# Two of four token tiles turned by VectorE's 32x32 blocks and a trip through DRAM: the second norm of a sparse-attention block

## The chip, the cores and the metric

The kernel runs on one core of a Trainium2 chip. The metric is the time of one execution on the device in microseconds, the median of several runs. The profile is one further execution, taken by the hardware profiler; its times are microseconds from the span's start.

## The reference

The block is a decoder layer for 512 tokens of width 2048: a mixer with native sparse attention, a SwiGLU FFN, an RMSNorm ahead of each and one at the end. What matters here lies between the mixer's output projection and the FFN's first product.

```python
def rmsnorm(x, g):
    y = x32 * lax.rsqrt(jnp.mean(x32 * x32, axis=-1, keepdims=True) + RMS_EPS)
    return (y * g.astype(jnp.float32)).astype(x.dtype)

h = h + nsa_mixer(hn, ...)             # ends in o @ w_out, o: 512 x 2048
h = h + swiglu(rmsnorm(h, ffn_norm_g[i]), ffn_w_in[i], ffn_w_out[i])
```

## The kernel before

**Numbers as two parts.** TensorE multiplies in a format with fewer bits than float32, so each operand is split into a high and a low part, and three products are added (`three`, L344 to L346). ScalarE makes the high part by a copy into the narrower format, VectorE the low part by a subtraction. Weights come in granules of 128x1024: SP loads a granule (L86), ScalarE copies it (L102), VectorE subtracts (L103). `W.take(n)` hands out the next granule and sees that n more are split; `W.ahead(n)` splits n granules ahead and issues the loads that follow. There are three raw and four split buffers, and extra places (`wr_h`, `wr_l`) for six granules.

**Order.** Every engine's instructions are written out in program order; nothing is scheduled for the kernel. An instruction that waits holds up all behind it on its engine. The queues for transfers are SP, ScalarE's and GpSimd's (POOL in the rows), each in order too.

**The output projection.** `acc` (128 tokens x 4 tiles x 2048) is loaded with x. The columns 1024 to 2047 are done first, in two column blocks of 512 (`cb` 2 and 3), for heads 0 to 11: six granules each, for each granule all four token tiles. Then `add` (L1030) adds the four PSUM banks to `acc`, and the spilled sums of the columns 0 to 1023 (`back`, from `d_h`) are added. Then comes the loop over the token tiles t, with heads 12 to 15: for each tile four column blocks of 12 products of 512 columns. `out_tiles` gives four banks, two from `psx` and two named `po`; each has one buffer, so a block writes the bank that the same block of the tile before (or of the column block before) had, and must wait until VectorE's `add` has read it.

**The second norm.** In that loop each block's columns are squared and summed (ScalarE, L1086), the residual is stored to `d_r` by GpSimd (L1082), the factor of each token comes from `rstd` (six small steps, VectorE and one square root on ScalarE), and `scaled` (L314) multiplies by the factor and by ffn_g (`gb2`, ffn_g on all partitions) into the one buffer `xn`. TensorE turns `xn` in the next tile's column blocks 1 and 2, eight 128x128 transposes each (`turned`, L322), so that the 2048 channels lie on partitions; ScalarE (L328) and VectorE (L333) split the result out of PSUM into `n2_hl`. Tile 3 is turned in the first FFN products, which begin with the tokens of tiles 0 and 1.

`ready_made` is a generator of transfers on GpSimd's queue: it makes sums of FFN weights in DRAM (`d_w`), by turns two plain copies of 512 KB and two that accumulate onto them.

The attention turns its probabilities in another way, which the change uses for two tiles: VectorE turns each 32x32 block (L919), four SP transfers write to DRAM with the blocks in a new place (L921), one reads them back (L925).

Of the kernel before, what the change touches and what calls it, by code (L numbers as in the profile page):

```python
# [10 lines left out]
F32 = mybir.dt.float32  # L11
F32R = mybir.dt.float32r
I32 = mybir.dt.int32
AF = mybir.ActivationFunctionType
OP = mybir.AluOpType
# [4 lines left out]
S, D, H, DH, G, HPG = 512, 2048, 16, 128, 4, 4  # L20
NT, KC = S // 128, D // 128
# [6 lines left out]
N_SPILL = 4  # L28
NF = DFF // 128
N_PLAIN = 3  # L30
N_TAIL = 4
G1, G2 = tuple(range(1, 11)), tuple(range(11, 21))
PASSES = [(0, (7, 8, 9, 10, 1, 2, 3, 4, 5, 6), (6, 7, 8, 9, 10)),
# [123 lines left out]
def granules(w_in, w1k, w1v, w_out, f_in, f_out):  # L157
# [46 lines left out]
    off.update((len(out) + i, 0) for i in range(4))  # L204
    for p in range(N_PLAIN):
        out += [(4, 256, [(0, 256, mat(f_in, 512 * i, 4, ffn_col(p), 256, 2 * DFF))]) for i in range(4)]
# [9 lines left out]
def nsa_block(ctx: ExitStack, tc: tile.TileContext, x, rel_bias, mix_g, ffn_g, fin_g, w_in, w_out,  # L216
              pos_k, w1k, w2k, pos_v, w1v, w2v, f_in, f_out, onehot, out):
    nc = tc.nc
    mm, act, dve, pool = nc.tensor.matmul, nc.scalar.activation, nc.vector, nc.gpsimd
# [6 lines left out]
    dram = ctx.enter_context(tc.tile_pool(name="dram", bufs=1, space=DRAM))  # L226
# [5 lines left out]
    W = Weights(nc, rawp, convp, specs)  # L232
    W.at, W.off = 48, off

    ident = const.tile([128, 128], F32, name="ident")
# [6 lines left out]
    d_o = [dram.tile([4, 128, S], F32, name=f"d_o{i}") for i in range(3)]  # L242
    d_h = dram.tile([S, 256 * N_SPILL], F32, name="d_h")
    d_r = dram.tile([NT, 128, D], F32, name="d_r")
    d_a = dram.tile([NF // 2, 128, 5 * S], F32, name="d_a")
    d_w = {j: dram.tile([128, 4, 2, 256], F32, name=f"d_w{j}") for j in G1 + G2}

# [32 lines left out]
    ready_made = made_ahead()  # L280

    def tok(t):
        return slice(128 * t, 128 * (t + 1))
# [22 lines left out]
    def rstd(ss):  # L306
        y = smallp.tile([128, 1], F32, name="rs")
        run(rstd_steps(ss, y))
        return y

    def scaled(src, y, gb, dst):
        for j in range(4):
            c = slice(512 * j, 512 * (j + 1))
            dve.scalar_tensor_tensor(dst[:, c], src[:, c], y, gb[:, c], op0=OP.mult, op1=OP.mult)  # L314
# [112 lines left out]
    with ExitStack() as st1:  # L427
# [11 lines left out]
        with ExitStack() as st0:  # L439
# [86 lines left out]
            p = bank([128, 512])  # L526
            for i in range(N_WARM):
                nc.tensor.transpose(p[:, 128 * (i % 4):128 * (i % 4 + 1)], ident, ident)
            p = bank([128, KC])
# [29 lines left out]
            for q in range(4):  # L559
# [23 lines left out]
                if q == 3:  # L583
                    p = bank([128, S])
# [100 lines left out]
        for i in range(8):  # L685
            g = W.take()
            for t in range(NT):
# [4 lines left out]
                if i == 7:  # L692
                    act(ge[:, t], ps[t][:, 256:304].rearrange("p (n h) -> p n h", n=3), AF.Exp,
                        scale=yneg[:, t:t + 1])
                    v_out(ps[t][:, :256], t, VV[0][0][:, t], VV[0][1][:, t])
            if i == 1:
                p = ps1.tile([128, 128], F32, name="tr")
# [27 lines left out]
        p = ps1.tile([96, G, 128], F32, name="tr")  # L725
# [293 lines left out]
    n2_hl = hn_t  # L1019
    resid = ctx.enter_context(ExitStack())  # L1020
    accp = resid.enter_context(tc.tile_pool(name="accp", bufs=1))
    ps3 = early.enter_context(tc.tile_pool(name="ps3", bufs=4, space=PSUM, side="right"))
    acc = accp.tile([128, NT, D], F32, name="acc")
# [20 lines left out]
    with tc.tile_pool(name="n2", bufs=1) as n2:  # L1044
        act(warm, epsc, AF.Sqrt)
        gb2 = n2.tile([128, D], F32, name="gb2")
        nc.scalar.dma_start(gb2, ffn_g[0:1, :].to_broadcast([128, D]))
        xn = n2.tile([128, D + 64], F32, name="xn")
        wr_h = n2.tile([128, 6, 1024], F32R, name="wr_h")
        wr_l = n2.tile([128, 6, 1024], F32R, name="wr_l")  # L1050
        for i in range(6):
            W.place[marks[0] + i] = wr_h[:, i], wr_l[:, i]
        for cb in (2, 3):
            po = out_tiles()
            cs = [slice(256 * c, 256 * (c + 1)) for c in (2 * cb - 4, 2 * cb - 3)]
            parts = [n2.tile([128, 1024], F32, name="back", bufs=3).rearrange("p (t c) -> p t c", t=NT) for _ in cs]
            for i in range(6):
                if i == 2:
                    for c, p in zip(cs, parts):
                        nc.sync.dma_start(p, d_h[:, c].rearrange("(t p) c -> p t c", p=128))  # L1060
                w = W.take(2 if cb == 2 else min(2 + i, 6))
                for t in range(NT):
                    tokmajor(po[t], w, heads(i), i == 0, i == 5, t)
            W.ahead(3)
            for t in range(NT):
                add(t, cb, po[t])
            for c, p in zip(cs, parts):
                dve.tensor_tensor(acc[:, :, c], acc[:, :, c], p, op=OP.add)
        w8 = []
        for t in range(NT):  # L1070
            ss = smallp.tile([128, 4], F32, name="ss4")
            po = out_tiles()
            for cb in range(4):
                for i in range(2):
                    if t == 0:
                        w8.append(W.take(7 - len(w8)))
                    tokmajor(po[cb], w8[2 * cb + i], heads(6 + i), i == 0, i == 1, t)
                add(t, cb, po[cb])
                if t == NT - 1 and cb == 3:
                    W.ahead(3)  # L1080
                if cb == 3:
                    pool.dma_start(d_r[t], acc[:, t])  # L1082
                if t and cb in (1, 2):
                    turned(xn, (2 * cb - 2, 2 * cb - 1), t - 1)
                junk = ps3.tile([128, 512], F32, name="pp")
                act(junk, acc[:, t, 512 * cb:512 * (cb + 1)], AF.Square, accum_out=ss[:, cb:cb + 1])  # L1086
            next(ready_made)
            scaled(acc[:, t], rstd(ss), gb2, xn)
            W.ahead(min(t, 2))
        firstp.close()  # L1090
        pf0 = ctx.enter_context(tc.tile_pool(name="pf0", bufs=2, space=PSUM))
        pa = [ps3.tile([128, 512], F32, name="pp") for _ in range(2)]
        gs = []
        for i in range(4):
            gs.append(W.take(min(2, 3 - i)))
            run(ws(pa, i, gs[i], 0, 256, of=n2_hl))
            if i in (1, 2):
                turned(xn, (2 * i - 2, 2 * i - 1), 3)
        act(warm, epsc, AF.Silu)
# [94 lines left out]
    def load_unit(q):  # L1194

        p, u = N_PLAIN + q // 2, q % 2
        v = []
# [62 lines left out]
    def merge(p):  # L1260

        A, B, C, F = banks.pop(p)
        p += N_PLAIN
        e = E[p] = ep.tile([128, 6, 256], F32, name="E")
# [15 lines left out]

    NQ = 2 * (2 * NF // 2 - N_PLAIN)
    with tc.tile_pool(name="tmp", bufs=1) as tmp:
# [7 lines left out]
        for i in range(4):  # L1290
            run(ws(pa, i, gs[i], 256, 512, start=False, end=end, of=n2_hl))
            W.ahead(min(i + 1, 3))
            some(1 if i < 3 else 2)
        for p in range(N_PLAIN):
            if p:
                pa = [ps3.tile([128, 512], F32, name="pp") for _ in range(2)]
                end = plain_out(p, pa)
                for i in range(4):
                    w = W.take()
                    if i == 0 or i == 2 and p < N_PLAIN - 1:  # L1300
                        next(ready_made)
# [9 lines left out]
        for u in range(2):  # L1311
            k = slice(8 * u, 8 * u + 4)
# [105 lines left out]
    ss = [late2.tile([128, 4], F32, name=f"sf{t}") for t in range(NT)]  # L1418
# [59 lines left out]
    def tail_load(i):  # L1478

        n = NU - N_TAIL + i  # L1480
        a_hl[n] = [x[:, 48:48 + 2 * S] for x in (slot_tile(), slot_tile())]
        nc.sync.dma_start(f32(a_hl[n][1]), d_a[UNITS[n][1]][:, :1024])

    def tail_split(i):
        h, l = a_hl[NU - N_TAIL + i]
        act(h, f32(l), AF.Copy)
# [69 lines left out]
    for s, (b, js, _) in enumerate(PASSES):  # L1556
# [6 lines left out]
        for i, j in enumerate(units):  # L1563
            left = len(units) - 1 - i
            if n + 3 < NU - N_TAIL:
                load_x(n + 3)
            load_form(n)
            if pending is not None:
                o = accb["now"] = late2.tile([128, NT, 512], F32, name="accb")
# [42 lines left out]
        if last_pass:  # L1612
            two = [slot_tile(F32)[:, 48:1072].rearrange("p (t c) -> p t c", t=2) for _ in range(2)]
            merge_sums(pending, two)
            acc = [x[:, t] for x in two for t in range(2)]
            continue
        o = accb["now"]
# [53 lines left out]
    for t in range(NT):  # L1671
# [16 lines left out]
        y = rstd(ss[t])  # L1688
# [39 lines left out]
```

## Time and profile before

| | us |
|---|---|
| median of 3 runs | 2101.22 |
| lowest, highest | 2100.24, 2101.4 |
| the profiled execution's own time | 2101.66 |
| its span, first to last instruction | 2099.9 |
| TensorE busy in it | 2077.9 |
| VectorE busy | 1627.9 |
| ScalarE busy | 948.8 |

The mean granted TensorE clock is 0.998 of full speed. Products are pipelined: the time from the start of one to the start of the next is what it costs, not its duration.

### The profile page before, as it was taken

Reading aid. Unit: us, or ns where it says so; the run is one execution under the profiler, and the core shown is the slowest. Engines: PE = TensorE matmul, PEld = TensorE weight load, DVE = VectorE, ACT = ScalarE, POOL = GpSimd, SP = SyncE. Lnnn points to the kernel's source line nnn. Section 1 sums busy time; section 2 is a strip of 40 time slices with the busy share of each in tenths; the row PEclk is TensorE's granted clock in tenths of the full one; section 3 lists DMA queues with packets and bytes.
Section 4 is the critical chain, followed back from the end, with each engine's and each line's share of the span. In section 5 each row is a group of like instructions: output and inputs, shape, how many; then the busy total and the mean of one; then the engine's idle time right before and its main releaser. Section 6 shows DMA issues by size and latency. Waiting matters only on the chain.

```text
span 2099.9 us, 39086 instructions
## 1 busy us (share of the span) xinstructions
PE 2077.9 (99%) x15239; PEld 1954.7 (93%) x15239; DVE 1627.9 (78%) x2705; ACT 948.8 (45%) x1524; POOL 279.8 (13%) x406
## 2 busy tenths in 40 slices
PE   9999999999989999999999999999999999999998
PEld 7898788898979889899999999999999999999997
DVE  5565777777787357898888888888888688697767
ACT  5344455555555334434434344344343465464445
POOL 2000111111101001022222132221211100000000
PEclk9999999999999999999999999999999999999999
DMA  7555667666777658578878778788755686685667
GB/s 232 183 150 153 186 190 197 193 192 192 204 221 210 242 171 221 152 203 236 212 205 227 204 223 221 193 236 209 198 158 156 209 267 184 191 298 152 193 204 278
DMA packets 320902, 427.68 MB, mean 204 GB/s; under 512 B 39787, under 2 KB 248875, under 8 KB 320076
## 3 DMA queue, kind: packets, MB, share of 16 engines
q1 hardware_dynamic: 259964, 291.65, 44.3%
q0 software_dynamic: 59856, 131.69, 26.0%
q8 instruction: 119, 1.95, 0.4%
q10 hardware_dynamic: 896, 1.84, 0.2%
q14 instruction: 67, 0.55, 0.1%
HBM read 363.12 MB, written 130.13 MB: 235 GB/s over the span
## 4 chain that ended last, share of the span: by engine, by line
PE 67%; DMA 1%; DVE 1%; ACT 0%; issue 0%; SPq 0%; DVEq 0%; ACTq 0%
PE f L345 18%; PE f L344 18%; PE f L346 18%; PE proj L344 2%; PE proj L346 2%; PE proj L345 2%; PE pp L345 1%; PE pp L346 1%; PE pp L344 1%; PE po L344 1%; PE po L345 1%; PE po L346 1%; DMA tlo<-d_w 1%; PE pp L322 0%; DMA tlo<-in_ffn_w_out 0%; DMA gt<-in_final_norm_g 0%
## 5 line engine op out<-in xcount | busy, mean ns | idle before, releaser
L103 DVE TENSOR_TENSOR wlo<-raw,whi 128x1024 fp32r<-128x1024 f32 (+2 forms) x223 | 247.4, 1111 | 122.9 <-ACT whi L102 122.4
L102 ACT ACTIVATE whi<-raw 128x1024 fp32r<-128x1024 f32 (+2 forms) x223 | 215.9, 971 | 219.9 <-PE f L346 62.2
L344 PE MATMUL f<-hn_h,whi 128*128 128x256 f32 x984 | 271.6, 276 | 0.0
L346 PE MATMUL f<-hn_h,wlo 128*128 128x256 f32 x984 | 271.6, 276 | 0.0
L345 PE MATMUL f<-hn_l,whi 128*128 128x256 f32 x984 | 271.6, 276 | 0.0
L1220 ACT ACTIVATE whi<-raw 128x1024 fp32r<-128x1024 f32 x123 | 126.1, 1057 | 303.0 <-DVE raw L1116 299.6
L1116 DVE TENSOR_TENSOR tlo<-tt,thi 128x1536 fp32r<-128x1536 f32 (+1 forms) x83 | 145.4, 1752 | 77.3 <-ACT thi L1225 77.1
L344 PE MATMUL proj<-hn_h,whi 128*128 128x512 f32 x512 | 204.2, 399 | 0.7 <-ACT hn_h L486 0.7
L345 PE MATMUL proj<-hn_l,whi 128*128 128x512 f32 x512 | 200.6, 392 | 0.3 <-DVE hn_l L487 0.3
L346 PE MATMUL proj<-hn_h,wlo 128*128 128x512 f32 x512 | 200.6, 392 | 0.0
L345 PEld LDWEIGHTS f<-hn_l,whi 128*128 128x128 f32 x984 | 184.7, 188 | 0.0
L344 PEld LDWEIGHTS f<-hn_h,whi 128*128 128x128 f32 x984 | 184.7, 188 | 0.0
L346 PEld LDWEIGHTS f<-hn_h,wlo 128*128 128x128 f32 x984 | 184.7, 188 | 0.0
L1225 ACT ACTIVATE thi<-tt 128x1536 fp32r<-128x1536 f32 x82 | 121.8, 1486 | 72.9 <-PE f L345 61.3
L344 PE MATMUL f<-thi,slot 128*128 128x256 f32 (+1 forms) x546 | 152.0, 278 | 0.0
L345 PE MATMUL f<-tlo,slot 128*128 128x256 f32 (+1 forms) x546 | 152.0, 278 | 0.0
L346 PE MATMUL f<-thi,slot 128*128 128x256 f32 (+1 forms) x546 | 151.9, 278 | 0.0
L346 PE MATMUL proj<-whi,hn_l 128*128 128x256 f32 (+2 forms) x496 | 145.4, 293 | 3.8 <-DVE hn_l L807 3.8
L1116 DVE TENSOR_TENSOR wlo<-raw,whi 128x1024 fp32r<-128x1024 f32 x123 | 147.0, 1223 | 1.1 <-ACT whi L1220 1.1
L344 PE MATMUL proj<-whi,hn_h 128*128 128x256 f32 (+2 forms) x496 | 145.7, 294 | 0.8 <-ACT hn_h L806 0.8
L345 PE MATMUL proj<-wlo,hn_h 128*128 128x256 f32 (+2 forms) x496 | 144.8, 292 | 0.0
L345 PE MATMUL f<-wlo,slot 128*128 128x256 f32 (+1 forms) x432 | 121.7, 282 | 0.0
(400 smaller groups left out, 6452.1 us busy)
## 6 DMA issues: line engine op xcount, KB each, us to landing
raw<-in_ffn_w_in SPq DMA_DIRECT2D x135, 512.0 KB, 5.3
d_w<-in_ffn_w_out POOLq DMA_DIRECT2D x80, 512.0 KB, 8.5
rawx<-in_ffn_w_in SPq DMA_DIRECT2D x41, 512.0 KB, 5.4
raw<-in_ffn_w_out SPq DMA_DIRECT2D x73, 256.0 KB, 3.8
tlo<-d_w SPq DMA_DIRECT2D x73, 256.0 KB, 4.5
d_a<-d_a POOLq DMA_DIRECT2D x120, 128.0 KB, 6.0
slot<-d_a SPq DMA_DIRECT2D x18, 768.0 KB, 7.5
raw<-in_nsa_w_in POOLq DMA_DIRECT2D x24, 512.0 KB, 5.0
```

The source lines that it names most:

```text
L102: self.nc.scalar.activation(hi[:, :n], src, AF.Copy)
L103: self.nc.vector.tensor_tensor(lo[:, :n], src, hi[:, :n].bitcast(F32), op=OP.subtract)
L344: mm(o, ah, bh, start=start, stop=False, skip_group_check=True)
L345: mm(o, ah, bl, start=False, stop=False, skip_group_check=True)
L346: mm(o, al, bh, start=False, stop=stop, skip_group_check=True)
L1116: dve.tensor_tensor(o, a, b, op=OP.subtract)
L1220: act(h, r, AF.Copy)
L1225: act(h, ttf, AF.Copy)
```

## The change

For token tiles 0 and 1 `turned` and `scaled` are left out. Instead ScalarE copies the tile of `acc` into `xn`, times the token's factor, with the columns in a new order; VectorE turns all 32x32 blocks of `xn` in place; four SP transfers of 256 KB write it to `d_n`, and one of 1 MB reads it back over the tile's part of `acc`, now with channels on partitions. Two tiles later, in column blocks 1 and 2, `landed_split` makes the two parts, eight channel blocks of 128 at a time, one instruction of ScalarE and one of VectorE for each, both times ffn_g, which is a factor of each partition now (`gcol2`). That column is loaded as 16 rows of 128 and turned by TensorE after column block 2 of the first part. Four of the steps of `ready_made` move from the ends of the token tiles to the granules 3 and 5 of the two column blocks. `W.ahead(min(t, 2))` at the end of each tile gives way to one `W.ahead(2)` in tile 0, before its factor is made.

```diff
+BLOCKED = 2
...
+    d_n = [dram.tile([4, 32, 4, 512], F32, name=f"d_n{t}") for t in range(BLOCKED)]
...
         xn = n2.tile([128, D + 64], F32, name="xn")
+        gcol2 = xn[:, D:D + KC]
+        nc.scalar.dma_start(xn[:KC, :128], ffn_g.rearrange("o (k p) -> (o k) p", p=128))
+
+        def blocked(t, y):
+
+            act(xn[:, :D].rearrange("p (m k j) -> p k m j", m=4, j=32),
+                acc[:, t].rearrange("p (k m j) -> p k m j", m=4, j=32), AF.Copy, scale=y)
+            dve.transpose(xn[:, :D], xn[:, :D])
+            for a in range(4):
+                nc.sync.dma_start(d_n[t][:, :, a].rearrange("m j f -> j m f"),
+                                  xn[32 * a:32 * a + 32, :D].rearrange("j (m f) -> j m f", m=4))
+            nc.sync.dma_start(acc[:, t], d_n[t].rearrange("m j a f -> (m j) (a f)"))
+
+        def landed_split(t, ks):
+
+            v = acc[:, t].rearrange("p (a k s) -> p k a s", a=4, s=32)
+            h, l = (x[:, :, tok(t)].rearrange("p k (a s) -> p k a s", a=4) for x in n2_hl)
+            for k in ks:
+                act(h[:, k], v[:, k], AF.Copy, scale=gcol2[:, k:k + 1])
+                dve.scalar_tensor_tensor(l[:, k], v[:, k], gcol2[:, k:k + 1], h[:, k].bitcast(F32),
+                                         op0=OP.mult, op1=OP.subtract)
+
...
             for i in range(6):
+                if i in (3, 5):
+                    next(ready_made)
...
             W.ahead(3)
+            if cb == 2:
+                gp = ps3.tile([128, 512], F32, name="pp")
+                nc.tensor.transpose(gp[:, :KC], xn[:KC, :128], ident[:KC, :KC])
+                dve.tensor_copy(gcol2, gp[:, :KC])
             for t in range(NT):
                 add(t, cb, po[t])
...
-                if t and cb in (1, 2):
+                if t > BLOCKED and cb in (1, 2):
                     turned(xn, (2 * cb - 2, 2 * cb - 1), t - 1)
                 junk = ps3.tile([128, 512], F32, name="pp")
                 act(junk, acc[:, t, 512 * cb:512 * (cb + 1)], AF.Square, accum_out=ss[:, cb:cb + 1])
-            next(ready_made)
-            scaled(acc[:, t], rstd(ss), gb2, xn)
-            W.ahead(min(t, 2))
+                if 2 <= t < 2 + BLOCKED and cb in (1, 2):
+                    landed_split(t - 2, range(8 * cb - 8, 8 * cb))
+                if not t and cb == 3:
+                    W.ahead(2)
+            y = rstd(ss)
+            if t < BLOCKED:
+                blocked(t, y)
+            else:
+                scaled(acc[:, t], y, gb2, xn)
```

## Rows read from the trace of the kernel before

**Rows 1.** The page, busy us, share of the span and instructions.

```profile
PE 2077.9 (99%) x15239; PEld 1954.7 (93%) x15239; DVE 1627.9 (78%) x2705; ACT 948.8 (45%) x1524; POOL 279.8 (13%) x406
```

**Rows 2.** TensorE's waits, whole span: instruction <- releaser: us, times, longest.

```profile
PE proj L346 <- DVE hn_l L807: 3.8, 4, 2.2
PE o L344 <- issue: 3.1, 1, 3.1
```

**Rows 3.** Timeline of TensorE, token tiles: start, us, engine, line, operation.

```profile
760.66 0.39 PE L344 MATMUL proj<-wr_h,hn_h 128*128 128x512 f32 x1
...
771.54 0.39 PE L344 MATMUL proj<-wr_h,hn_h 128*128 128x512 f32 x1
...
776.98 1.03 PE L322 MATMUL pp<-ident,xn 128*128 128x128 f32 x8
...
784.20 0.39 PE L344 MATMUL proj<-wr_h,hn_h 128*128 128x512 f32 x1
...
797.10 0.39 PE L344 MATMUL proj<-wr_h,hn_h 128*128 128x512 f32 x1
```

**Rows 4.** Timelines: the second column block's start on three engines; a 16-row transpose.

```profile
713.70 1.06 ACT L102 ACTIVATE whi<-raw 128x1024 fp32r<-128x1024 f32 x1 [6.18 <-DMA raw<-in_nsa_w_out]
...
725.01 1.28 DVE L1030 TENSOR_TENSOR acc<-acc,proj 128x512 f32<-128x512 f32 x2
...
728.02 0.39 PE L344 MATMUL proj<-whi,hn_h 128*128 128x512 f32 x1
...
5.85 0.23 PE L530 MATMUL mlp<-ident,g 16*128 16x16 f32 x1
...
6.12 0.17 DVE L531 COPY gcol<-mlp 128x16 f32<-128x16 f32 x1 [4.91 <-PE mlp L530]
```

**Rows 5.** Timeline of VectorE around the end of token tile 0.

```profile
763.73 2.35 DVE L103 TENSOR_TENSOR wlo<-raw,whi 128x1024 fp32r<-128x1024 f32 x2
...
773.21 0.16 DVE L293 TENSOR_REDUCE ms<-ss 128x1 f32<-128x4 f32 x1 [0.79 <-ACT pp L1086]
...
774.67 2.74 DVE L314 SCALAR_TENSOR_TENSOR xn<-acc,rs,gb 128x512 f32<-128x512 f32 x4
```

**Rows 6.** Groups by shape, whole span: count, busy us, mean ns, idle before.

```profile
L1691 ACT ACTIVATE slot<-slot,rs 128x1024 f32<-128x1024 f32 x3 | 3.5, 1152 | 2.6 <-DVE rs L304 2.6
...
L919 DVE STREAM_TRANSPOSE p<-p 128x1152 f32<-128x1152 f32 x16 | 22.1, 1379 | 0.6
L919 DVE STREAM_TRANSPOSE p<-p 128x896 f32<-128x896 f32 x16 | 17.8, 1112 | 0.5
...
L942 ACT ACTIVATE pth<-ptr 128x128 fp32r<-128x128 f32 x32 | 9.3, 297 | 4.3 <-DMA ptr<-d_p 4.3
...
L906 ACT ACTIVATE p<-u,mx 128x128 f32<-128x128 f32 x32 | 12.4, 387 | 0.0
...
L946 DVE TENSOR_TENSOR ptl<-ptr,pth 128x128 fp32r<-128x128 f32 x32 | 9.1, 284 | 21.5 <-ACT pth L942 21.5
```

**Rows 7.** Transfers: SP and GpSimd timelines, issues (KB, median us to landing), a window.

```profile
682.32 1.75 SPq L921 DMA_DIRECT2D d_p<-p  x4
687.73 0.52 SPq L925 DMA_DIRECT2D ptr<-d_p  x1
...
772.72 0.56 POOL L1082 DMA_DIRECT2D d_r<-acc  x1 [78.63 <-DVE acc L1030]
...
d_w<-in_ffn_w_out POOLq DMA_DIRECT2D x80, 512.0 KB, 8.5
...
d_r<-acc POOLq DMA_DIRECT2D x4, 1024.0 KB, 5.4
...
gb<-in_ffn_norm_g ACTq DMA_DIRECT2D x1, 1024.0 KB, 8.4
...
704.00:706.00 2.00, 2.00 (x10) 1.68 (x9) 0.00 (x0) 0.00 (x0) 0.00 (x0) 1.00 1.00 416
```

**Rows 8.** A 1 us window after TensorE's longest wait: busy by engine, granted clock, DMA.

```profile
222.00:223.00 1.00, 1.00 (x4) 0.76 (x3) 0.47 (x2) 0.00 (x0) 0.45 (x1) 0.50 0.93 308
```

## The prediction

> **What bounds the kernel now.** I read the page's busy times first: TensorE works 99% of the span [rows 1], so the kernel lasts as long as TensorE's instruction stream plus its waits. The list of TensorE's waits over the span comes next: eight groups, 13.4 us in all, of which the two longest stand in [rows 2]; none lies between 740 and 850 us, where the change works. So an instruction taken out of TensorE there is worth its whole time, and a wait put in costs its whole time. Last came the timeline from 760 to 823 us, by engine. Token tile 0, which turns nothing, takes 771.54 - 760.66 = 10.88 us; tile 1, which turns tile 0, 12.66; tile 2, 12.90 [rows 3]. VectorE and ScalarE have idle time there, but the reader must look at their order, not their share: each takes its instructions in the order in which the kernel writes them, and an add that frees a PSUM bank or a factor that TensorE needs can stand behind an instruction that waits for something else.
>
> **What is removed.** Two tiles' transposes, four sets of eight. By the lengths of the tiles that is (12.66 - 10.88) + (12.90 - 10.88) = 3.8 us of TensorE time. All of it is on the path. The eight copies out of PSUM and the eight VectorE scalings that go with it are hidden today and count for nothing by themselves.
>
> The Trainium skill speaks against this trade: "VectorE: DVE Perf Modes", section "Rules for kernel authors", sends a 128x128 transpose to TensorE if a PSUM destination will do, because VectorE turns 32x32 blocks only. No run before shows the full turn on VectorE; the page gives no time for the detour.
>
> **The ffn_g column.** One 16-row transpose on TensorE after the second column block's products, and a copy of it to SBUF on VectorE ahead of that block's four adds. The same pair at the start of the kernel took 0.23 and 0.17 us [rows 4]. Its place matters more than its length. Today the first add starts at 725.01, while TensorE is still at that block's later tiles, so all banks are free when the next block starts at 728.02. In the new order the add waits for a transpose that comes after all four tiles. The next block's tile 0 writes the bank that this add empties (one buffer for each of the four). So: transpose to 728.3, copy, add from 728.45 for 0.64, TensorE goes on at 729.15, or 1.1 us later than now. Below, the bound is the transpose alone, 0.2; above, 1.4 if copy and add don't overlap. I take 1.1, since the order fixes it.
>
> **The early accumulating DMAs.** Four steps of ready_made (eight DRAM transfers of 512 KB) move from the token tiles into the two column blocks. GpSimd's queue waits from 772.72 - 78.63 = 694 us with nothing in it, so they start there, in a stretch where the DMA engines are already full [rows 7], beside x, the spilled partial sums and w_out. The granule that the next block starts on is converted at 713.70 as soon as it has landed, and is needed at 728.02 [rows 4]; that cover of some 12 us hides them. I cost them at nothing; without the cover it is a rival.
>
> **The new chain, tile 0.** Times are on the old clock, without the 1.1 us. Today the sum of squares is reduced at 773.21 and the factor is there at 774.67 [rows 5]. The change puts two ffn_w_in splits ahead, one conversion of 1.06 [rows 4] and then two subtractions, 2.35 [rows 5], less what overlaps, so the reduction starts at 776.5 and the factor is there at 778.0. ScalarE's scaled copy of 128x2048 is twice the 1152 ns of the 128x1024 row, less one start: 2.1 us (1.9 to 2.3 [rows 6]). The block transpose by VectorE's two rows is 1379 + 896 x 267/256 ns, 2.31 us; 2.45 if it scaled with size [rows 6]. It ends at 782.6. Then four writes of 256 KB on SP. In the attention four writes of the same form and the read behind them were issued 5.4 us apart [rows 7]; I take 5.5, up to the 8.4 of a 1 MB load in a full stretch, not under 4.9. The read of 1 MB back: 5.4, as the store of 1 MB; 4.9 to 8.4 [rows 7]. Tile 0 lands at 793.6. The two ffn_w_in loads that the splits set free stand on SP ahead of the writes and are issued before 778; behind the writes SP has nothing that TensorE needs before tile 3 is over. The store of the residual, which reads the same tile, is issued at 772.72 and takes 5.4 [rows 7], so it holds back nothing.
>
> **Who stands behind it.** VectorE waits for the copy and turns from 778.1 to 782.6, and tile 1's four adds are queued behind that. TensorE would start tile 2 at 771.54 + 10.88 = 782.4 in the bank of tile 1's first add, which ends at 783.3: a wait of 0.9 us.
>
> Tile 1's last add ends at 785.1, its factor is there at 787.5. Its scaled copy writes the same buffer xn, which the four writes free at 788.1; copy to 790.2, transpose to 792.6. Tile 2's first two adds, ready since 786 and 789, are done only at 793.8. Now the split of tile 0, in two halves of eight channel blocks. The nearest rows are ScalarE's 128x128 copies of 297 ns (387 with a per-partition operand) and VectorE's 284 ns [rows 6]; consecutive ones overlap, so I take 0.30 a step, ends 0.22 and 0.39, and VectorE one step behind. The half ends at 797.3. Then, one behind the other: add, square, second half to 801.5, add, square, factor (1.5) to 804.4, and two of the four scalings, 1.4: tile 2's first half of xn is there at 805.8. Today the same half is there at 774.67 + 1.37 = 776.0, and TensorE asks at 776.98 [rows 3, 5]. TensorE asks after tile 3's second block, at 783.3 + 10.88 + 5.44 = 799.6. It waits 6.2 us.
>
> Then the same in small: tile 3's adds and tile 1's split follow the late scaling. The first half of tile 1 ends at 812.9, add and both subtractions of the turned blocks free the bank of the first FFN product at 814.9; TensorE is there at 813.1 and waits 1.8. The second half, add, a split, square, factor and half a scaling end at 821.7; TensorE, two granules further (as many columns each as a block, 2.72), is at 820.3 and waits 1.4. Sum of waits 0.9 + 6.2 + 1.8 + 1.4 = 10.3 us.
>
> **The sum.** -3.8 + 1.1 + 10.3 = +7.6 us. The profiled execution took 2101.66 for its span of 2099.9, so 2109.3; it lies 0.4 above the median of 2101.22, so I forecast 2108.8. With steps of 0.22, DMA times of 4.9 and a copy of 1.9 the waits, walked again, make 6.7 and the sum is +4.0; with steps of 0.39, the read at 8.4, a copy of 2.3 and a turn of 2.45 they make 15.7 and the sum is +13.0. The read is not what binds at 5.4 (tile 0 lands 0.9 before ScalarE turns to it); at 8.4 it adds some 2 us.
>
> **Rivals.** 0.2%, 4.2 us, is about what a measurement of this kernel can tell from no change.
>
> Forecast, waits of serial work on VectorE and ScalarE: 2105.2 to 2114.2, chance 0.65, of which 0.04 under +4.2.
>
> Cover holds: the turns on VectorE delay nobody because the scaling of tile 2 comes in time. What it needs is its first half by 799.6, or 6.2 us sooner than I count. For it speaks that tile 0's DMA trip ends before its use; against it, that every step of the chain behind 792.6 has a row. Price: -3.8 + 1.1, or 2098.5, same. Chance 0.13. That the column's wait doesn't come either and a little more than the sets is gained, 2097.0 or less: 0.07, the only case that is faster.
>
> DMA crowd: the moved transfers hold back the granules at 700 to 728. Each took 8.5 us [rows 7], and they go in four pairs, one pair behind the other, 34 us; if they get half of the engines meanwhile, what SP carries is late by up to 17 us, 5 more than the cover: 2113.8. Chance 0.08.
>
> Clock: after the one TensorE wait of 3.1 us [rows 2] the granted clock stood at 0.50, the 1.2 GHz level, for three slices of 1 us and a part of two more [rows 8]: 3 x 0.50 and 0.2, 1.7 us of work lost. A 6.2 us wait should bring this too. I leave it out of the sum since it falls ahead of the waits of 1.8 and 1.4, which take it up: TensorE only comes less early. If it isn't taken up, +9.3, 2110.5. Chance 0.07.
>
> The Trainium skill, "TensorE: Matmul & The Clock Gate", section "What's actually happening", says the same of the cause: the throttled state is the default and activity releases it. The row agrees, with 0.50 after the wait.
>
> **Chances and range.** Faster 0.07; same 0.13 + 0.04 = 0.17; slower 0.61 + 0.08 + 0.07 = 0.76. The range goes from 2101.5, about half the way from the forecast's low end to the held cover, since a part of the cover can hold, to the forecast's high end of 2114.2. Left out are the two cases of a gain, 0.20.
>
> **What would show it.** TensorE's transposes of xn are 32 instead of 64, and the wait list gets three names between 728 and 830: an add on VectorE (about 1 us twice), a transpose waiting for xn's scaling (about 6), and the first FFN products (1 to 2, twice). The block transposes last 2.3 us, and tile 0's ends some 9 us behind that tile's last square. The granted clock falls once behind the long wait. Wrong would be: tile 2's scaling on time, no wait of over 1 us at the third turn; the trip through DRAM over 14 us; or waits on w_out at 728 to 760.

## The result and the profile after

The changed kernel takes 2118.65 us (median of 5 runs, 2117.42 to 2121.07) against 2101.22 of before: ratio 1.0084, 95% interval 1.0073 to 1.0095. That is slower, as forecast, but by 17.4 us instead of 7.6, and above the range. The profiled execution took 2117.98 us, its span is 2116.2.

The page's busy line of the changed kernel, to be held against [rows 1]:

```profile
PE 2080.3 (98%) x15208; PEld 1954.7 (92%) x15208; DVE 1630.5 (77%) x2724; ACT 958.2 (45%) x1550; POOL 279.5 (13%) x406
```

TensorE's waits of the changed kernel, the four longest groups (sum in us, times, longest). The first two don't stand in the list of before [rows 2]:

```profile
PE proj L346 <- DVE acc L1032: 9.2, 3, 7.7
PE pp L324 <- DVE xn L316: 6.3, 1, 6.3
PE proj L348 <- DVE hn_l L809: 3.1, 3, 2.2
PE o L346 <- issue: 2.7, 1, 2.7
```

Where they stand shows the timeline of TensorE, the first product of each stage with the wait ahead of it in brackets:

```profile
728.17 0.23 PE L1093 MATMUL pp<-ident,xn 16*128 16x16 f32 x1
736.15 0.77 PE L346 MATMUL proj<-whi,hn_h 128*128 128x512 f32 x1 [7.75 <-DVE acc L1032]
...
771.67 0.39 PE L346 MATMUL proj<-wr_h,hn_h 128*128 128x512 f32 x1
...
782.55 0.39 PE L346 MATMUL proj<-wr_h,hn_h 128*128 128x512 f32 x1
...
793.88 0.50 PE L346 MATMUL proj<-wr_h,hn_h 128*128 128x512 f32 x1 [0.29 <-DVE acc L1032]
...
806.28 0.50 PE L346 MATMUL proj<-wr_h,hn_h 128*128 128x512 f32 x1 [1.20 <-DVE acc L1032]
...
818.33 1.94 PE L324 MATMUL pp<-ident,xn 128*128 128x128 f32 x8 [6.27 <-DVE xn L316]
...
828.28 0.28 PE L346 MATMUL pp<-hn_h,whi 128*128 128x256 f32 x1
```

Up to 728 us TensorE runs alike in both kernels. Two losses follow, and the larger one lies ahead of the token tiles, in a stretch that the prediction held for nearly untouched:

- **Column blocks.** The token tiles start at 771.67 instead of 760.66 [rows 3]: 11.0 us. Of these 8.1 lie between the last product of the first column block and the first of the next (728.08 to 736.15, the wait of 7.75 with the 16-row transpose), and 2.9 in the block behind, which runs partly at the lower clock and takes 35.52 us instead of 32.64.
- **Token tiles.** 10.88, 11.33, 12.40 and 22.0 us, 56.6 in all, against 49.3 before, from 760.66 [rows 3] to the first FFN product below: 7.3 us, with the wait of 6.27 for xn that was forecast at 6.2.

```profile
810.00 0.28 PE L344 MATMUL pp<-hn_h,whi 128*128 128x256 f32 x1
```

The sum of the two, 18.3, and some 0.3 over the FFN's first granules make the 18.6 by which TensorE is late at 850 us. The span is only 16.3 longer, since between 1715 and 1775 us the profiled execution of before is itself 1.8 us slower than that of the changed kernel, and than that of eight of the kernels below, the one with the move alone and the one without turns among them. What slows it there isn't known.

The rows below show stretches of 2 us (time, busy us and count of TensorE, its weight loads, VectorE, ScalarE, GpSimd; then the granted clock, the DMA share, GB/s). The granted clock fell to 0.50, the 1.2 GHz level, during or behind each of the two long waits, as behind the one wait of before [rows 8]:

```profile
728.00:730.00 2.00, 0.40 (x3) 0.13 (x1) 0.00 (x0) 0.00 (x0) 0.37 (x1) 1.00 1.12 311
...
732.00:734.00 2.00, 0.00 (x0) 0.00 (x0) 0.72 (x1) 0.99 (x1) 0.00 (x0) 0.50 1.14 217
...
740.00:742.00 2.00, 2.00 (x6) 1.52 (x6) 1.20 (x2) 0.00 (x0) 0.00 (x0) 0.50 0.11 31
...
820.00:822.00 2.00, 2.00 (x7) 1.61 (x6) 1.36 (x3) 1.14 (x4) 0.00 (x0) 0.50 0.00 0
```

Why the first wait is so long stands in three views of the changed kernel. First GpSimd's timeline, the DMA issues from 693.5 to 712 us (KB each, median us to landing) and ScalarE's conversions of w_out:

```profile
694.12 0.66 POOL L256 DMA_DIRECT2D d_w<-in_ffn_w_out  x1
```

```profile
acc<-in_x SPq DMA_DIRECT2D x2, 2048.0 KB, 21.4
d_w<-in_ffn_w_out POOLq DMA_DIRECT2D x6, 512.0 KB, 14.8
...
back<-d_h SPq DMA_DIRECT2D x2, 512.0 KB, 24.0
...
raw<-in_nsa_w_out SPq DMA_DIRECT2D x1, 512.0 KB, 21.9
```

```profile
724.36 1.06 ACT L103 ACTIVATE whi<-raw 128x1024 fp32r<-128x1024 f32 x1 [16.78 <-DMA raw<-in_nsa_w_out]
730.40 1.06 ACT L103 ACTIVATE whi<-raw 128x1024 fp32r<-128x1024 f32 x1 [4.99 <-DMA raw<-in_nsa_w_out]
733.01 1.06 ACT L103 ACTIVATE whi<-raw 128x1024 fp32r<-128x1024 f32 x1 [1.55 <-DMA raw<-in_nsa_w_out]
```

SP's queue belongs to the picture, first of the kernel before and then of the changed one:

```profile
701.46 4.30 SPq L1060 DMA_DIRECT2D back<-d_h  x2
```

```profile
702.90 10.66 SPq L1086 DMA_DIRECT2D back<-d_h  x2
```

Then VectorE's timeline from 724 to 737 us:

```profile
725.45 1.23 DVE L104 TENSOR_TENSOR wlo<-raw,whi 128x1024 fp32r<-128x1024 f32 x1 [16.61 <-ACT whi L103]
731.49 1.23 DVE L104 TENSOR_TENSOR wlo<-raw,whi 128x1024 fp32r<-128x1024 f32 x1 [4.82 <-ACT whi L103]
734.10 1.22 DVE L104 TENSOR_TENSOR wlo<-raw,whi 128x1024 fp32r<-128x1024 f32 x1 [1.39 <-ACT whi L103]
735.24 0.17 DVE L1094 COPY xn<-pp 128x16 f32<-128x16 f32 x1
735.33 1.27 DVE L1032 TENSOR_TENSOR acc<-acc,proj 128x512 f32<-128x512 f32 x2
```

The moved transfers start at 694.12, and a 512 KB load of w_out issued beside them takes 21.9 us. SP is held for 10.66 instead of 4.30 us at the two loads of spilled sums, and the w_out loads behind them are issued from 713.7 us on instead of 705.9. The granule that the next block starts on is converted at 724.36 instead of 713.70 [rows 4] and its subtraction is over at 726.7: its own cover of 12 us did hold. But the splits look ahead. The two granules behind it are converted at 730.40 and 733.01, and their subtractions stand on VectorE ahead of the four adds. The first add begins at 735.33 instead of 725.01 [rows 4], and TensorE waits for the PSUM bank that it empties.

### The profile page after: what moved, and what is told of

It reads as the page before. It is cut to its first block, busy times and chain, and to the rows that moved or that the text cites. A ratio compares the mean times of both kernels' runs of the same rounds, so it can differ in the third digit from the quotient of the medians.

```text
span 2116.2 us, 39098 instructions
## 1 busy us (share of the span) xinstructions
PE 2080.3 (98%) x15208; PEld 1954.7 (92%) x15208; DVE 1630.5 (77%) x2724; ACT 958.2 (45%) x1550; POOL 279.5 (13%) x406
## 4 chain that ended last, share of the span: by engine, by line
PE 62%; issue 2%; DVE 2%; DMA 2%; SPq 1%; ACT 1%; POOL 0%; ACTq 0%; DVEq 0%; POOLq 0%
PE f L347 19%; PE f L346 19%; PE f L348 18%; PE pp L348 1%; PE pp L347 1%; PE pp L346 1%; PE proj L346 1%; PE proj L347 1%; PE proj L348 1%; DMA raw<-in_nsa_w_out 1%; SPq L1086 1%; PE po L346 0%; PE po L347 0%; PE po L348 0%; SPq L87 0%
```

## The experiments

All ratios are against the kernel before, run on the same chip beside each group. "Shift" is by how much TensorE runs behind the profiled execution of before, read by laying the two lists of products side by side.

**Undo the move.** The four `next(ready_made)` out of the column blocks, back to the tile ends:

```diff
-                if i in (3, 5):
-                    next(ready_made)
...
+            next(ready_made)
             y = rstd(ss)
```

> The changed kernel with the four steps of ready_made put back at the ends of the token tiles. Theory 1 (the moved transfers make the w_out granules late, and the adds stand behind the late granules' splits on VectorE): TensorE's wait of 7.7 us at 728 shrinks to the 1.1 us of the ffn_g column's order, and the granted clock stays full there, so 2118.6 - 11.0 + 1.1 = 2108.7 us; up to 2112 if the transfers, back among the tiles, lengthen the trip through DRAM. Rival (the wait comes from the column's transpose and copy ahead of the adds): it stays, 2115 us or more.

2113.97 us, ratio 1.0061 (1.0046 to 1.0076): 4.7 won, not 10, and 2 above what the theory allowed. The column blocks cost only 1.4 now (shift 0.7 at 725 us, 2.1 at 750). But the transfers now run beside the trip through DRAM. ScalarE's and VectorE's timelines of this kernel, and TensorE's wait:

```profile
801.12 2.45 ACT L1069 ACTIVATE hn_h<-acc,xn 128x128 fp32r<-128x128 f32 x8 [3.48 <-DMA acc<-d_n]
```

```profile
801.56 2.39 DVE L1070 SCALAR_TENSOR_TENSOR hn_l<-acc,xn,hn_h 128x128 fp32r<-128x128 f32 x8 [4.75 <-ACT hn_h L1069]
```

```profile
811.90 1.94 PE L324 MATMUL pp<-ident,xn 128*128 128x128 f32 x8 [9.90 <-DVE xn L316]
```

The split of tile 0 waits for its tile to land, and the wait for xn grows from 6.27 to 9.90. So the move does shelter the trip, and pays for it in w_out.

**The move alone,** in the kernel before (the same lines with the signs turned, nothing else):

> The kernel before with only the four steps of ready_made moved into the column blocks; tiles are turned by TensorE as before. Theory 1: the wait at 728 and the fall of the clock come with the move alone, so 2101.2 + 10.5 = 2111.7 us (2109 to 2113). Rival (the wait needs the column's transpose and copy): no change, 2101.2 us, within 1 us.

2109.89 us, ratio 1.0049 (1.0032 to 1.0065): 9.1 us from eight transfers whose data no instruction of this stretch reads. TensorE's longest wait of this kernel, and the order of VectorE:

```profile
735.33 0.76 PE L344 MATMUL proj<-whi,hn_h 128*128 128x512 f32 x1 [6.26 <-DVE acc L1030]
```

```profile
733.36 1.23 DVE L103 TENSOR_TENSOR wlo<-raw,whi 128x1024 fp32r<-128x1024 f32 x1 [1.04 <-ACT whi L102]
734.50 1.28 DVE L1030 TENSOR_TENSOR acc<-acc,proj 128x512 f32<-128x512 f32 x2
```

It is the same picture without the ffn_g column or the turns. The theory holds, and the rival (the column's transpose and copy) falls.

**The adds ahead** of the splits and the ffn_g column, in the changed kernel:

```diff
+            for t in range(NT):
+                add(t, cb, po[t])
             W.ahead(3)
             if cb == 2:
...
-            for t in range(NT):
-                add(t, cb, po[t])
```

> The changed kernel with the four adds of each column block ahead of the split of further granules and ahead of the column's copy; the transfers stay moved. Theory 1 with order as the cause: x lands at 717 and TensorE's first tile is done at 724.5, so the adds run from 725 and the wait of 7.7 us and the clock's fall go: 2118.6 - 11 = 2107.7 us. Rival (the granules themselves are too late for TensorE): a wait on a split of w_out takes its place, 2113 us or more.

2115.29 us, ratio 1.0068 (1.0053 to 1.0083): the direction of the theory, a third of the size, and a time in the rival's range. VectorE's timeline of this kernel:

```profile
731.79 1.23 DVE L104 TENSOR_TENSOR wlo<-raw,whi 128x1024 fp32r<-128x1024 f32 x1 [5.28 <-ACT whi L103]
732.93 1.28 DVE L1032 TENSOR_TENSOR acc<-acc,proj 128x512 f32<-128x512 f32 x2
```

One late subtraction still stands ahead: that of the lookahead inside the block's last `W.take(2)`, not of `W.ahead(3)`. The wait falls from 7.75 to 4.67. Order explains 3 us here; the rest is the late granule, through the subtraction that still stands ahead.

**No turns.** The kernel before without the transposes and splits of tiles 0 and 1, whose tokens the FFN then doesn't get:

```diff
-                if t and cb in (1, 2):
+                if t > 2 and cb in (1, 2):
```

> The kernel before with the turns of tiles 0 and 1 and their two splits left out, so that the FFN's first half works on tokens that were not normalised; nothing is put in their place. It prices the gain by itself. By the tile lengths: 3.8 us less, 2097.4 us. Rival (part of the transposes' time is covered): 2099 us or more.

2097.81 us, ratio 0.9987 (0.9977 to 0.9996). From 775 to 800 us and on the shift goes from 2.16 to -1.55, 3.7 us; the medians differ by 3.0. That is all that the change can win.

**Transfers in the quiet stretch.** They wait behind a GpSimd copy that reads an accumulator column of the first column block's last tile; adds first:

```diff
+            if cb == 2:
+                gate = smallp.tile([128, 1], F32, name="gate")
+                pool.tensor_copy(gate, acc[:, NT - 1, 512 * cb:512 * cb + 1])
+                for _ in range(4):
+                    next(ready_made)
```

> The changed kernel with both harms of the column blocks taken away: the eight accumulating transfers wait (behind one small GpSimd copy that reads the accumulator) until the adds of the first column block are done, and so run in 728 to about 765 us, where neither x nor the spilled sums nor the DRAM trip is under way; and the four adds stand ahead of the split and of the ffn_g column. Theory (the 11.0 us lost ahead of the token tiles are the crowd at 694 and the adds behind the late granules; the 7.3 us in the tiles are serial work on VectorE and ScalarE): only the tiles' part is left, 2100.8 + 7.5 + 0.2 = 2108.5, range 2106 to 2110.5, with no TensorE wait over 1 us at 728 and the wait for xn still near 6.3. Rival (the crowd only moves, the stretch behind 728 isn't quiet enough): 2113 or more, with waits on granules between 728 and 771.

2124.04 us, ratio 1.0111 (1.0096 to 1.0126), far from both. At 850 us the shift is 8.8, about the theory's 7.7; then it grows by 0.35 in every 25 us of the FFN. Three variants that ran beside it had the same new tile: with two idle buffers for tile 1; on top of that with both splits in tile 3; and on top of that with the factors on GpSimd and splits of 512 columns. Their main lines, in this order:

```diff
+            if t:
+                bs = [n2.tile([128, 1024], F32, name="back", bufs=3) for _ in range(2)]
...
-                if 2 <= t < 2 + BLOCKED and cb in (1, 2):
-                    landed_split(t - 2, range(8 * cb - 8, 8 * cb))
+                if t == NT - 1:
+                    landed_split(cb // 2, range(8 * (cb % 2), 8 * (cb % 2) + 8))
...
+            pool.tensor_tensor(v, v, gcol2.unsqueeze(1).unsqueeze(3).to_broadcast([128, 4, KC, 32]), op=OP.mult)
```

> As the gated kernel, but tile 1 is scaled and turned in two idle 128x1024 buffers instead of in xn, so ScalarE no longer waits 4.2 us for the four writes of tile 0; each write becomes two halves. Theory A (the wait for xn is serial work only): the turn of tile 1 ends some 4 us sooner and the wait of 6.3 falls to about 2, 2104.3. Theory B (tile 0's trip through DRAM is next in line: it lands at 795 on the clock of before, while the split would then be asked for at 790.5): half of it comes back as a wait for the landing, 2106.5. Range of both 2103 to 2108.5. If nothing is won (2108.5), the buffer was no link of the chain.

> As the kernel with two buffers, but both tiles' splits stand in token tile 3, behind tile 2's scaling: eight channel blocks in each of its four column blocks. Theory (VectorE's serial work is what binds): tile 2's scaling comes in time and the wait for xn goes; but tile 3 now has 2.75 + 2.6 + 2.6 + 9.8 = 17.7 us of VectorE work against 12.7 of TensorE, so about 6 us come back as waits of the first FFN products: 2100.8 - 3.8 + 6 = 2103, range 2099 to 2107. Rival (the splits fit beside tile 3): 2097 to 2098, faster than before. Second rival (something else than the splits holds back xn): the wait of some 6 us stays, 2108.

> As the kernel with both splits in token tile 3, but the ffn_g factors are applied to the landed tiles by GpSimd in one multiplication each, so that a split is four wide pairs (512 columns) instead of sixteen narrow ones: 5.1 us of VectorE work in tile 3 instead of 9.8. Theory (serial VectorE and ScalarE work binds): the waits of the first FFN products shrink from about 6 to about 3, for the landing of tile 1 and GpSimd's pass over it, 2100.8 - 3.8 + 3 = 2100, range 2097 to 2104. Rival: GpSimd's pass takes longer than 6 us or slows VectorE, and the kernel is no faster than the one with narrow splits.

They took 2120.33, 2124.08 and 2121.08 us (ratios 1.0102, 1.0103 and 1.0096; the four times of the second lie in two pairs, near 2120 and 2128), and for them too only the traces up to 850 us tell something: shifts of 4.9, 13.6 and 4.9. In the second the wait for xn at tile 3 is gone, and waits of 1.68, 1.23 and 2.53 stand behind it, as that theory says; 5.95 more stand at 768 us, behind a w_out granule that ScalarE waited 5.81 for; this was the slowest of its four executions. In the third the factors on GpSimd stop VectorE, as its timeline and GpSimd's show:

```profile
796.93 0.16 DVE L300 RECIPROCAL rs<-rs 128x1 f32<-128x1 f32 x1 [0.27 <-ACT rs L298]
797.13 2.94 DVE L302 SCALAR_TENSOR_TENSOR nt<-rs,ms 128x1 f32<-128x1 f32 x1
```

```profile
796.39 3.67 POOL L1073 TENSOR_TENSOR acc<-acc,xn 128x2048 f32<-128x2048 f32 x1
```

A 128x1 instruction that takes 0.22 us elsewhere lasts 2.94 and ends at 800.07, when GpSimd's multiplication does (800.06). The Trainium skill, "SBUF — State Buffer", section "SBUF: two separate sides", says why: VectorE and GpSimd share a pair of ports, and where a VectorE instruction with two SBUF inputs meets a GpSimd instruction that reads SBUF, the first holds it for its whole instruction and the other is blocked. The rows agree: the blocked one reads `rs` and `ms`, while the reciprocal ahead of it, with one input, took its 0.16 us beside the same multiplication.

**The new tile taken out, and put in alone.** The gate copy now writes an unused column of xn; the same with two buffers; and the kernel before with nothing but an unused tile:

```diff
-                pool.tensor_copy(gate, acc[...])
+                pool.tensor_copy(xn[:, D + 32:D + 33], acc[...])
```

```diff
+    pad = smallp.tile([128, 1], F32, name="pad")
+    pool.memset(pad, 0.0)
```

> The gated kernel again, but GpSimd's small copy goes into an unused column of xn instead of a new 128x1 tile (three buffers, 12 bytes per partition). In the first gated run TensorE stood only 8.8 us behind the kernel before at 850 us, and then lost 0.35 us more in every 25 us of the FFN, with no wait and a granted clock of 1.00. Theory (the new tile moved all later buffers by 12 bytes, and that alone slows the FFN's products): without it the time is 2100.8 + 8.8 = 2109.5, range 2107.5 to 2111.5. Rival (the gated transfers themselves slow the FFN): again about 2124.

> As the gated kernel without the new tile, with two idle 128x1024 buffers for tile 1. In the first such run TensorE stood 4.9 us behind before at 850 us. Theory (ScalarE's wait for tile 0's writes is a link of the serial chain, and nothing else of the change costs): 2100.8 + 4.9 = 2105.7, range 2104 to 2107.5. Rival (the gain of 3.9 is given back later): as the gated kernel, 2109.

> The kernel before, unchanged in all its work, with one unused 128x1 tile (three buffers, 12 bytes per partition) set to zero at the start. Theory (12 bytes of displacement slow the FFN's products by 1.3%): 10.5 us between 890 and 1680 us and some 3 more behind, 2114, range 2110 to 2117. Rival (the drift came from the gated transfers): 2100.8, within 1.5.

All three came as the theories had them: 2110.17 (ratio 1.0051, 1.0034 to 1.0068), 2105.28 (1.0019, 1.0010 to 1.0029) and 2115.96 us (1.0072, 1.0057 to 1.0087). The unused tile, twelve bytes per partition, costs 15 us. The window from 1200 to 1300 us, first of the gated kernel without the tile, then of before with it:

```profile
1200.00:1300.00 100.00, 100.00 (x885) 100.00 (x884) 86.03 (x103) 42.46 (x42) 22.69 (x31) 1.00 0.85 218
```

```profile
1200.00:1300.00 100.00, 100.00 (x873) 100.00 (x872) 86.32 (x104) 38.15 (x37) 23.37 (x35) 1.00 0.74 205
```

885 products against 873 in the same time, both at a clock of 1.00 and without a wait. Laid beside the kernel before, from 890 to 1700 us, the loss of 10.8 us stands almost whole in the 3012 products that read the buffers thi and tlo: 10.35 us, 3.4 ns each. The 4038 others lose 0.5 together.

Against the changed kernel, the gate and the adds' place give back 8.5 us by the medians. The quiet stretch isn't always quiet: in the profiled execution of the gated kernel, the slowest of its five, one w_out granule was late and TensorE waited 6.61 at 770.84. The second buffer gives back 4.9 more: ScalarE scales tile 1 at 786.42 without waiting for tile 0's writes, and the wait for xn falls to 3.98.

**Another order.** From the two-buffer kernel: the turn behind the next tile's second add, tile 0's split in blocks (2, 2) and (3, 0) (tile, block), tile 1's from (3, 2) on and between the quarters of tile 3's scaling, `W.ahead(3)` in tile 3 left to the next take:

```diff
-                if 2 <= t < 2 + BLOCKED and cb in (1, 2):
-                    landed_split(t - 2, range(8 * cb - 8, 8 * cb))
...
+                for tt, cc, b, ks in ((2, 2, 0, range(8)), (3, 0, 0, range(8, KC)), (3, 2, 1, range(4)), (3, 3, 1, range(4, 8))):
+                    if (t, cb) == (tt, cc):
+                        landed_split(b, ks)
+                if t in (1, 2) and cb == 1:
+                    turn(t - 1)
```

> As the kernel with two buffers, with the instructions of VectorE and ScalarE put in another order and no work taken out: the block transpose of a tile stands behind the next tile's second add instead of ahead of its first, the two ffn_w_in splits behind tile 0's scaled copy and turn, and tile 0's split in the third block of tile 2 and the first of tile 3, tile 1's from the third block of tile 3 on and between the quarters of tile 3's scaling. Theory (it is the order of the two queues that costs, not the amount of work up to tile 3): tile 2's scaling is there at 798.4 on the clock of before, asked for at 798.7, so the wait for xn goes; in tile 3 VectorE has 16.5 us of work and some 3 come back as waits of the FFN's first products: 2100.8 - 3.8 + 3 = 2100, range 2097 to 2104. Rival (the amount of work binds wherever it stands): 2105, as the kernel with two buffers.

2108.02 us, ratio 1.0034 (1.0023 to 1.0045): slower than the kernel it came from. Half of the expectation held: no wait for xn is left. But TensorE's timeline has others in its place:

```profile
816.38 0.66 PE L324 MATMUL pp<-ident,xn 128*128 128x128 f32 x4 [2.77 <-DVE hn_l L335]
...
831.81 0.58 PE L348 MATMUL pp<-hn_h,wlo 128*128 128x256 f32 x1 [3.06 <-DVE wlo L104]
```

The clock falls to 0.50 behind each, and the tiles cost 7.2 (shift 10.2 at 775 us, 17.4 at 850), more than with two buffers alone (3.2). The profiled execution is the slowest of nine, 2117.19 us, with one more late granule (a wait of 5.36 at 768.74) ahead of the tiles.

**Transfers in the FFN.** The two-buffer kernel without the gate; the four steps go beside others in the FFN's product units:

```diff
-        for _ in range(PRE[q % len(PRE)]):
+        for _ in range(PRE[q % len(PRE)] + (q in (2, 4, 6, 8))):
```

> The kernel with two buffers, but the four moved steps of ready_made (eight DRAM transfers) go into neither the column blocks nor the token tiles: each is issued beside another step early in the FFN's product units. In the gated kernels single executions had a w_out granule late beside them (6.6 and 5.4 us of wait at 769). Theory: with the transfers out of the way no granule of w_out is late, the column blocks cost 0.2 to 0.4 and the tiles 3.2 to 3.7: 2104.5, range 2102.5 to 2106.5, and a narrower spread than 2103 to 2110. Rival (the transfers only do their harm elsewhere): granules of ffn_w_in late in the FFN, 2108 or more.

2104.54 us, ratio 1.0016 (1.0007 to 1.0025), eleven runs between 2102.9 and 2106.4: the expected time to 0.1, and no w_out granule late. The column blocks cost 0.4 (shift 0.58 at 725 us, 1.01 at 750), and 3.6 are left in the tiles, with a wait for xn of 4.39.

**One tile.** `BLOCKED = 1` on top of that, tile 0 in the idle buffers, its turn behind tile 1's second add, its split in blocks (2, 2) and (3, 0); then the second half moved to (3, 2):

```diff
-                if (t, cb) in ((2, 2), (3, 0)):
+                if (t, cb) in ((2, 2), (3, 2)):
                     landed_split(0, range(8) if t == 2 else range(8, KC))
```

> The change in half its size, with what the runs have taught: only token tile 0 is turned by VectorE's blocks and DRAM (in the two idle buffers), tile 1 by TensorE as before; the turn stands behind tile 1's second add; the adds stand ahead of splits and the ffn_g column; the transfers of ready_made as in the other kernel of this call. Two sets of transposes (1.9 us) are saved. Theory A (what costs is order, buffers and crowd, and VectorE has room for one tile's detour: 11.6 us of work in tile 3 against 12.7): 2100.8 - 1.9 + 0.4 = 2099.3, range 2097.5 to 2101, no wait for xn over 0.5. Theory B (the detour's serial work always costs more than the transposes): 2102.5 or more, with a wait for xn or an add of over 2 us.

> The kernel with one tile, with one thing moved: the second half of tile 0's split stands behind tile 3's third block instead of its first. In the run with one tile everything up to 800 us was as theory A has it (1.2 us ahead of before, or 2.0 less the 0.8 of the column blocks), and then that half-split stood on VectorE between tile 3's first two adds and the subtractions that free the PSUM bank of the third block's transposes: a wait of 2.7, and 1.4 more at the lower clock behind it. Theory A: with the half-split behind those subtractions, where VectorE then stood idle for 2.7, the wait goes: 2105.5 - 4.1 + 0.4 = 2101.8 by that kernel's own median, 2099.7 by the sum over before; range 2098.5 to 2102.5. Theory B (the work costs wherever it stands): the wait comes back at the next product, 2105, range 2104 to 2107.

2105.54 (ratio 1.0022, 1.0013 to 1.0031) and 2102.76 us (1.0009, 1.0000 to 1.0018). The first came in the time of its theory B, though with a wait on another instruction than that names, a subtraction. TensorE's timeline has the wait that the half-split causes:

```profile
808.24 0.66 PE L324 MATMUL pp<-ident,xn 128*128 128x128 f32 x4 [2.70 <-DVE hn_l L335]
```

Moving eight pairs of instructions by two blocks takes it away and wins 2.8 by the medians. In the second the tiles win their two sets in full: the shift goes from 1.97 at 775 us to 0.01 at 825, with no wait of TensorE there. Yet the median is 3.1 above the sum of 2099.7 and 1.0 above the 2101.8 by the earlier kernel's median, just outside the range, and above that of before. In its profiled execution 1.5 us were lost ahead of 690 us and 0.7 around 1715 to 1725, and neither is explained; at 690 us the traces of all these kernels, alike up to there, lie between -1.4 and 3.0. No version here that does all of the work beats the kernel before.

## Why the prediction was wrong

**The step that failed: the early accumulating DMAs, costed at nothing.** The prediction named the crowd, where it starts (694) and one granule's cover of 12 us, and concluded that this cover hides the transfers. The cover was right for that granule. The work that is late is another: the adds, which stand on VectorE behind the splits of later granules. The move alone costs 9.1 us, nearly the whole of what the forecast lacks (17.4 measured, 7.6 forecast). The prediction's own rule, that an add can stand behind an instruction that waits, was applied to the token tiles and not to the column blocks. As the rival "DMA crowd" it was priced at 5 us, too low by the clock and by the adds' place, and given 0.08.

**The column, 1.1 us.** With the transfers undone the column blocks cost 1.4 by the trace, the upper bound; with the adds put first and the transfers in the FFN 0.4. So the order costs 1.0, about what was said.

**The sets removed, 3.8 us.** Right: 3.7 by the trace of the kernel without them.

**The new chain.** Sizes of the changed kernel from ScalarE's, VectorE's and SP's timelines:

```profile
788.90 2.01 ACT L1056 ACTIVATE xn<-acc,rs 128x2048 f32<-128x2048 f32 x1 [0.87 <-DVE rs L306]
801.30 2.01 ACT L1056 ACTIVATE xn<-acc,rs 128x2048 f32<-128x2048 f32 x1 [4.19 <-DMA d_n<-xn]
807.56 2.44 ACT L1069 ACTIVATE hn_h<-acc,xn 128x128 fp32r<-128x128 f32 x8
```

```profile
790.94 2.31 DVE L1058 STREAM_TRANSPOSE xn<-xn 128x2048 f32<-128x2048 f32 x1 [2.08 <-ACT xn L1056]
```

```profile
793.28 2.71 SPq L1060 DMA_DIRECT2D d_n<-xn  x4
801.27 0.34 SPq L1062 DMA_DIRECT2D acc<-d_n  x1
```

The factor comes 17.2 us after the tiles start (forecast 17.3), the copy takes 2.01 (2.1), the turn 2.31 (2.31), eight split steps 2.44 (2.4). The writes take 8.0 (5.5): the term that was too small, though inside its bound of 8.4. In the two-buffer kernel with the transfers in the FFN, writes and read are issued 5.5 apart for tile 0 (781.35 and 786.87), the forecast's figure, but 7.9 for tile 1 (789.62 and 797.51). What sets the difference isn't shown.

**Who stands behind it.** Forecast waits 0.9, 6.2, 1.8 and 1.4; measured 0.29 and 1.20 for the bank, 6.27 for xn, none at the first FFN product, some 0.3 in the granules behind it. The clock's fall behind the long wait was left out, since it would be taken up by the waits of 1.8 and 1.4. That came: these two went, but for the 0.3 at the FFN's start, and the fall costs nearly what they would have. Tile 3 takes 22.0 - 6.27 = 15.7 us beside its wait, against some 12.9 of a tile with its turns before [rows 3], 2.8 more. So the tiles and the FFN's start cost 7.6 where 6.5 had been summed (-3.8 and 10.3): the right mechanism, and an error of 1. It lies in the waits for the bank: tiles 1 and 2, now without turns, take 11.33 and 12.40 where 10.88 was counted, 2.0 in all instead of 0.9.

**The links.** That ScalarE's wait for xn is one of them the prediction said (tile 1's copy "writes the same buffer xn, which the four writes free"); a second buffer wins 4.9. That the waits are serial work, not the landing, holds for the changed kernel, whose splits never wait for a tile to land (the row at 807.56 has no wait). With the early transfers put back they do.

**What stays open.** Whether the detour can pay. With one tile the tiles' own stretch wins all of its 2.0 us, but the whole time doesn't show it. Two tiles, with the cures that were tried, weren't brought below 2104.5. A second PSUM buffer for the first adds wasn't tried.

## What to carry to other kernels

When transfers are moved to an empty queue, look at which loads they meet and follow each late load through all that is queued behind its consumers: here an instruction that needs none of the late data stood behind it in its engine's order. A cover has to be shown for every instruction behind the late one, lookahead included, and not for the first user alone. Price a long wait of TensorE with the slow clock behind it: here the two long waits, 7.75 and 6.27, cost 2.9 and 2.8 more.

## What the runs showed that was not expected

Twelve bytes of SBUF per partition, allocated early and never used again, slow the kernel before by 0.7%: products of the FFN run at 873 instead of 885 in 100 us, at a granted clock of 1.00. No view names a cause; that it is the address of the buffers is inferred from the edit, and from the loss standing in the products of two buffers. Whoever adds a tile for an experiment should first run the tile alone.

A GpSimd multiplication of 128x2048 (3.67 us) held a 128x1 VectorE instruction for 2.94 us. And a 512 KB load beside the moved DRAM transfers took 21.9 us, where those of before had 11.6 in the median in the same stretch, and 5.5 from 690 to 860 us.
